# A hybrid decoder layer: two pairs' first products computed ahead of the feed-forward, and pools laid out anew

## The chip, the cores and the metric

The kernel runs on one core of a Trainium2 chip. The metric is the device time of one launch in microseconds (us), as the median of several runs. Four compute engines matter. PE (TensorE) multiplies matrices, and its weight loads (PEld) overlap it. DVE (VectorE), ACT (ScalarE) and POOL (GpSimd) work on elements. SP's queue issues the transfers between HBM and the on-chip memory.

## The reference

The layer works on x of 1024 tokens by 1024 features, in float32:

```python
h = h + jnp.concatenate([o_gla, o_mla], axis=-1) @ w_out[l]      # two groups of heads
h = h + xo.reshape(b, s, XA_HEADS * XA_HEAD_DIM) @ xa_w_o[l]     # attention over 256 memory tokens
fn = rms_norm(h, norm_ffn[l])
g = fn @ ffn_w_gate[l]                                           # 1024 x 2816
g_pad = jnp.pad(g, ((0, 0), (CONV_W - 1, 0), (0, 0)))
cw = ffn_conv_w[l]
g_conv = ffn_conv_b[l] + sum(cw[i] * g_pad[:, i:i + s] for i in range(CONV_W))
h = h + (jax.nn.silu(g_conv) * (fn @ ffn_w_up[l])) @ ffn_w_down[l]
```

## The kernel before

**Arithmetic.** A float32 product is made of three fast ones. Each operand is split into a high part (an ACT copy to the fast type) and a low part (a DVE subtraction), and PE adds low times high, high times low and high times high. `split` does the two halves, `mm3` and `product` the three matmuls.

**Order of stages.** Input projections, gated linear attention and latent attention fill the span to about 483 us, w_out follows, and from about 575 to 717 us runs the cross-attention, a software pipeline over eight tiles of 128 tokens (`for s_ in range(NB + 5)`). Its last stages per tile are `x_o` (output product), `x_fn` (RMS norm) and `x_ft` (transposes and first sums). The feed-forward follows, and from about 1168 us the product with ffn_w_down (`dn`).

**The feed-forward product.** Gate (m_ = 0) and up (m_ = 1) are computed for 11 pairs j of 128-column blocks with a Winograd form of Strassen's scheme, which takes seven block products P1 to P7 instead of eight. The activation's halves are split by features (b1., b2.) and by tokens (tiles 0 to 3, tiles 4 to 7). P1 and P2 use tiles 0 to 3 alone (`fh`, `fl`). P5, P6, P7, P3 and P4 use tiles 4 to 7, and their operands `obP3` to `obP7` are combinations: t1 = b12 - b11 and t2 = b22 - t1 in `x_ft`, t2 - b11 (P7) and t2 - b21 (P4) in `x_t34`. For tiles 4 to 6 these sums run on POOL, for tile 7 on DVE (the variable `ge`). So nothing but P1 and P2 can start before the last tile is through the norm and all its combinations.

**P1 and P2 of pair 0** are therefore computed while the last tiles are worked on, from a separate load of the weights' first 128 columns (`w_first`, tiles hgate, lgate, hup, lup; PSUM tile `A2`, named A).

**The weights** of a pair come as two 1 MB loads (`raw_load`, tile `rw`, one for gate and one for up). `prep` makes the sums of blocks (tile `ss`; on DVE for the first, on POOL for all others) and splits each operand into a tile `op`, seven products ahead (`LA = 7`), in a ring of nine. `run` issues the product's 12 matmuls of 128x512 and adds its result to `GU`. Results of P1 are kept in `p1`.

**What sets the order.** The framework's scheduler orders each engine's instructions by dependences and priority; `pri` shifts the priority. SBUF tiles lie in pools which are stacked from the left and from the right. A tile waits until the last users of its place are done (`reuse_waits="tile"`). So `rw` of the up weights, in pool `rw1`, and the feed-forward's `ss` and `op` tiles wait for the cross-attention's tiles under them.

**Addresses.** The left pools begin 128 bytes past a multiple of 512, because the tile `xsrow` (128 bytes per partition) lies ahead of them. The right pools begin 160 bytes past one, because of the `padr` tile. In the pool of the projections' weights, tiles of 2432 bytes put those behind them at other places again.

Of the kernel before, what the change touches and what calls it, by code (L numbers as in the profile page):

```python
# [33 lines left out]
def build(tc, a, out):  # L34
# [315 lines left out]
    for k in range(KD):  # L350
        raw = xpc.tile([P, 304], F32, name="raw_wv1", tag="raw", bufs=5)
        nc.sync.dma_start(out=raw[:, 0:272], in_=a["w_in"][k * P:(k + 1) * P, C_V + 256:C_OG])
        nc.sync.dma_start(out=raw[:, 272:304], in_=a["w_in"][k * P:(k + 1) * P, C_PE:C_END])
        if k % 2 == 0:
            hi, lo = [pAc.tile([P, 2, 304], F32R, name=f"{nm}_wv1", tag="w", bufs=8) for nm in ("hi", "lo")]
        split(hi[:, k % 2], lo[:, k % 2], raw, col(R_NM + k))
        W.append((hi[:, k % 2], lo[:, k % 2]))
    for t in range(NB):
# [737 lines left out]
        tt(hs, hs, o, ALU.add)  # L1096

    def x_fn(t):
        if not fg:
            fg.append(p4c.tile([P, D], F32, name="fgain"))  # L1100
            nc.sync.dma_start(out=fg[0], in_=a["norm_ffn"].partition_broadcast(P).rearrange("p o n -> p (o n)"))
# [17 lines left out]
    def x_ft(t):  # L1119
# [28 lines left out]
        for nm, src in (("P6", t2), ("P5", t1)):  # L1148
            act(OB[nm][0][:, :, cs], src, AF.Copy)
            tt(OB[nm][1][:, :, cs], src, f32(OB[nm][0][:, :, cs]), ALU.subtract, ge)  # L1150

    def x_t34(nm, t):
# [4 lines left out]
        ge = nc.vector if t == NB - 1 else nc.gpsimd  # L1157
        b = OB["P1" if nm == "P7" else "P2"]
        if t < NB - 1:
            x = p4c.tile([P, 4, P], F32, name="t3", tag="xpT", bufs=2)  # L1160
        else:
            if len(TT) < 2:
                TT.append(qtc.tile([P, 2, 4, P], F32, name="t3b", tag="uB", bufs=1))
            x = TT[1][:, int(nm == "P4")]
        tt(x, T2R[t], f32(b[0][:, :, cs]), ALU.subtract, ge)
        tt(x, x, f32(b[1][:, :, cs]), ALU.subtract, ge)
# [63 lines left out]
    for s_ in range(NB + 5):  # L1230
# [27 lines left out]
        if s_ == 10:
            xvp.__exit__(None, None, None)
            p1p = pool("p1", "right"); p1c = p1p.__enter__()  # L1260
            rwp = [pool("rw0", "right")]
            rwc = [rwp[0].__enter__()]
            raw_load(0, 0)
            for t in range(4, 7):
                x_t34("P7", t)
            W0, A2 = [w_first(i) for i in range(2)], [two(0, [P, 2, 512], "A2")]
            for t in range(4, 7):
                x_t34("P4", t)
            for m_ in range(2):
                product(A2[0][:, m_], W0[m_][0:4], "P1", True)  # L1270
            p1_copy(0)
        if s_ == 11:
            p1_copy(1)
            qps.__exit__(None, None, None)
            x_ft(7)
            for m_ in range(2):
                product(A2[0][:, m_], W0[m_][4:8], "P2", False)
            x_t34("P7", 7)
            x_t34("P4", 7)
    GU = k16([P, 2, 2, S], F32, "GU")  # L1280
# [12 lines left out]
    NP = NF // 2
    ORDER = ("P1", "P6", "P5", "P7", "P2", "P3", "P4")
    prods = [(j, m_, nm) for j in range(NP) for m_ in range(2) for nm in ORDER if j or nm not in ("P1", "P2")]
    OPS, SS, BK, CV = {}, {}, {}, {}

    def prep(j, m_, nm):
# [21 lines left out]
    def conv(f, i):  # L1320

        g_ = GU[:, 0, i]
        c = CV[f] = fcc.tile([P, S], F32, name="conv", tag="conv", bufs=2)
        act(c, g_, AF.Identity, scale=col(R_CW + 2 * NF + f), bias=col(R_CB + f))
        stt(c[:, 1:], g_[:, 0:S - 1], col(R_CW + NF + f), c[:, 1:], ALU.mult, ALU.add)
        stt(c[:, 2:], g_[:, 0:S - 2], col(R_CW + f), c[:, 2:], ALU.mult, ALU.add)
        act(c, c, AF.Silu)

    def run(j, m_, nm):
# [18 lines left out]
        if (nm == "P2" or (j == 0 and nm == "P7")) and m_ == 0:  # L1348
            act(Y[:, 0, 0:512], A2[0][:, 0], AF.Copy)
        if (nm == "P2" or (j == 0 and nm == "P7")) and m_ == 1:  # L1350
            tt(CV[2 * j][:, 0:512], CV[2 * j][:, 0:512], A2[0][:, 1], ALU.mult)
# [114 lines left out]
```

## Time and profile before

| | |
|---|---|
| median of 3 runs | 1414.21 us (1414.16 to 1415.16) |
| the profiled execution | 1413.37 us, span 1411.6 us |
| TensorE clock granted, mean of the span | 0.989 |
| busy PE | 1364.3 us (97%) |
| busy DVE, ACT, POOL | 848.5, 636.8, 231.8 us |

The profile shows one execution. "Busy" counts time in which an engine had an instruction; a matmul's duration includes the time in which it overlaps the next one, so of a row of matmuls the distance between starts (the pitch) tells the speed. Engine idle time carries the instruction that ended it. The granted clock is 1.00 at full speed (2.4 GHz) and 0.50 at half (1.2 GHz).

### The profile page before, as it was taken

To read this page: it belongs to the slowest core of one execution; us is meant where nothing else is said; L and a number is where in the kernel's file an instruction comes from. 1 tells how busy PE (TensorE), PEld (TensorE's weight loads), DVE (VectorE), ACT (ScalarE), POOL (GpSimd) and SP (SyncE) were. 2 spreads that over 40 slices of the span, in tenths; PEclk is the share of its full clock that TensorE was granted. 3 is DMA by queue.
4 is the path that set the end of the run, shared out by engine and by line. 5 is a ranking of instruction groups with operands and counts; after the bars stand their busy time and mean duration, and the time that the engine had idled before them with its cause. 6 is when DMAs were issued, how large, how long until landed. Compare 5 with 4: busy or idle time off the path is not lost.

```text
span 1411.6 us, 19224 instructions
## 1 busy us (share of the span) xinstructions
PE 1364.3 (97%) x7372; PEld 1136.2 (80%) x7372; DVE 848.5 (60%) x1607; ACT 636.8 (45%) x1314; POOL 231.8 (16%) x339
## 2 busy tenths in 40 slices
PE   8999999899999999999966999999999999999998
PEld 8977789788777787888854788888888888888887
DVE  6536785776785624677766766666666656225321
ACT  6424457777776603565433433333333344223220
POOL 0300001222231000000183333222333300000000
PEclk9999999999999999999987999999999999999999
DMA  7111010110001302201012222222222138346521
GB/s 217 47 46 30 9 38 20 53 60 27 2 11 65 135 19 86 76 28 48 31 60 90 90 90 80 70 90 90 90 90 75 45 126 292 109 176 236 180 104 60
DMA packets 69068, 116.11 MB, mean 82 GB/s; under 512 B 6505, under 2 KB 45552, under 8 KB 68976
## 3 DMA queue, kind: packets, MB, share of 16 engines
q1 hardware_dynamic: 68802, 114.82, 24.1%
q8 instruction: 58, 0.95, 0.3%
q14 instruction: 34, 0.28, 0.1%
q10 hardware_dynamic: 174, 0.06, 0.0%
HBM read 94.95 MB, written 19.92 MB: 81 GB/s over the span
## 4 chain that ended last, share of the span: by engine, by line
PE 76%; issue 12%; DVE 4%; POOL 3%; ACT 3%; DMA 2%; SPq 0%; ACTq 0%; DVEq 0%; POOLq 0%
PE dn L1428 6%; PE dn L1429 6%; PE dn L1427 6%; PE P L1212 6%; PE P L1213 6%; PE P L1214 6%; PE pj L88 4%; PE pj L89 4%; PE pj L90 4%; PE mo L756 3%; PE A L1213 3%; PE A L1212 3%; PE A L1214 3%; PE PTp L727 2%; PE S L88 2%
## 5 line engine op out<-in xcount | busy, mean ns | idle before, releaser
L1212 PE MATMUL P<-obP,op 128*128 128x512 f32 x352 | 138.9, 395 | 18.0 <-DVE op L69 12.6
L1214 PE MATMUL P<-obP,op 128*128 128x512 f32 x352 | 138.4, 393 | 0.0
L1213 PE MATMUL P<-obP,op 128*128 128x512 f32 x352 | 138.4, 393 | 0.0
L1427 PE MATMUL dn<-wd,gt 128*128 128x512 f32 x352 | 136.9, 389 | 0.0
L1428 PE MATMUL dn<-wd,gt 128*128 128x512 f32 x352 | 136.9, 389 | 0.0
L1429 PE MATMUL dn<-wd,gt 128*128 128x512 f32 x352 | 136.9, 389 | 0.0
L69 DVE TENSOR_TENSOR wd<-rd,wd 128x1024 fp32r<-128x1024 f32 x44 | 53.0, 1224 | 92.9 <-ACT wd L66 92.9
L66 ACT ACTIVATE op<-ss 128x512 fp32r<-128x512 f32 x88 | 54.8, 630 | 116.9 <-PE P L1214 77.5
L69 POOL TENSOR_TENSOR ss<-rw 128x512 f32<-128x512 f32 x42 | 54.6, 1321 | 268.3 <-DVE op L69 268.3
L69 DVE TENSOR_TENSOR op<-rw,op 128x512 fp32r<-128x512 f32 x62 | 65.5, 1058 | 51.8 <-ACT op L66 51.8
L1212 PEld LDWEIGHTS P<-obP,op 128*128 128x128 f32 x352 | 67.0, 190 | 34.0 <-DVE op L69 13.0
L66 ACT ACTIVATE wd<-rd 128x1024 fp32r<-128x1024 f32 x44 | 45.7, 1058 | 95.9 <-PE dn L1429 49.8
L1214 PEld LDWEIGHTS P<-obP,op 128*128 128x128 f32 x352 | 66.9, 190 | 14.0
L1213 PEld LDWEIGHTS P<-obP,op 128*128 128x128 f32 x352 | 66.9, 190 | 13.9
L1427 PEld LDWEIGHTS dn<-wd,gt 128*128 128x128 f32 x352 | 66.1, 188 | 13.8
L1428 PEld LDWEIGHTS dn<-wd,gt 128*128 128x128 f32 x352 | 66.1, 188 | 13.8
L1429 PEld LDWEIGHTS dn<-wd,gt 128*128 128x128 f32 x352 | 66.1, 188 | 13.5
L66 ACT ACTIVATE op<-rw 128x512 fp32r<-128x512 f32 x62 | 39.0, 631 | 83.7 <-PE P L1214 65.4
L69 DVE TENSOR_TENSOR op<-ss,op 128x512 fp32r<-128x512 f32 x88 | 61.2, 701 | 19.6 <-ACT op L66 18.7
L1212 PE MATMUL A<-fh,op 128*128 128x512 f32 x160 | 62.2, 389 | 0.0
L1213 PE MATMUL A<-fl,op 128*128 128x512 f32 x160 | 62.2, 389 | 0.0
L1214 PE MATMUL A<-fh,op 128*128 128x512 f32 x160 | 62.2, 389 | 0.0
(408 smaller groups left out, 3621.3 us busy)
## 6 DMA issues: line engine op xcount, KB each, us to landing
rd<-in_ffn_w_down SPq DMA_DIRECT2D x44, 512.0 KB
rw<-in_ffn_w_gate SPq DMA_DIRECT2D x11, 1024.0 KB
rw<-in_ffn_w_up SPq DMA_DIRECT2D x11, 1024.0 KB
gdr<-conv SPq DMA_DIRECT2D x22, 512.0 KB
rgd<-gdr SPq DMA_DIRECT2D x44, 256.0 KB
mraw<-in_xa_w_kv SPq DMA_DIRECT2D x16, 256.0 KB
hh<-in_x SPq DMA_DIRECT2D x2, 2048.0 KB
raw_wo<-in_w_out SPq DMA_DIRECT2D x8, 512.0 KB
```

The costliest lines, as they stand in the source:

```text
L66: nc.scalar.activation(out=o, in_=i, func=f, **kw)
L69: (eng or nc.vector).tensor_tensor(out=o, in0=x, in1=y, op=op)
L88: mm(o, lhsT=ll, rhs=rh, start=i == 0, stop=False)
L89: mm(o, lhsT=lh, rhs=rl, start=False, stop=False)
L90: mm(o, lhsT=lh, rhs=rh, start=False, stop=last and i == n - 1)
L756: mm(u.o[r, i], lhsT=V[:, k, x.h * MV:(x.h + 1) * MV], rhs=x.pT[b][:, k - k0], start=k == 0, stop=k == u.t)
L1212: mm(o, lhsT=wl, rhs=bh[:, k], start=start and k == 0, stop=False, **kw)
L1213: mm(o, lhsT=wh, rhs=bl[:, k], start=False, stop=False, **kw)
L1214: mm(o, lhsT=wh, rhs=bh[:, k], start=False, stop=k == 3, **kw)
L1427: mm(ob[b], lhsT=gl, rhs=wh, start=f == 0, stop=False)
L1428: mm(ob[b], lhsT=gh, rhs=wl, start=False, stop=False)
L1429: mm(ob[b], lhsT=gh, rhs=wh, start=False, stop=f == NF - 1)
```

## The change

1. Before the feed-forward, a second pair's P1 and P2 are computed too. `w_first` takes the pair as argument; for pair 1 it splits the weights into a 16 KB tile `wx`. Four products (48 matmuls) write two PSUM pairs `x1p`, and P1 and P1 + P2 are kept in `X1`. Pair 1's P1 and P2 are gone from `prods`, with their splits. The loads of `w_first` are issued at steps 8 and 9 of the cross-attention and after it, instead of at step 10.
2. `x_t34` becomes `x_t234` with an engine argument. P6's part for tiles 4 and 5 stays on POOL, and for 6 on goes to DVE. P7's and P4's parts run on DVE for every tile, in the order 7, 6, 5, 4, those of P4 for tiles 5 and 4 later than the rest.
3. Pools are opened in another order. Conv tiles and three `op` tiles lie in `fc`, `ss` in `fs`, the rest in `rg`. The ring has seven `op` tiles up to pair 2, nine after. The look-ahead is six products for pairs 0 and 1 and eight after.
4. `xsrow` lies inside `alr`, `padr` grows from 320 to 480 bytes, and the 2432-byte weight tiles become 2560 bytes. All SBUF tiles of 1 KB and more then begin at a multiple of 512 bytes.

```diff
-    padr.tile([P, 80], F32, name="padr", tag="padr", bufs=1)
+    padr.tile([P, 120], F32, name="padr", tag="padr", bufs=1)
...
-    xsrow = const.tile([P, NB, XH], F32, name="xsrow")
+    xsrow = alr[:, :, 0:XH]
...
-            hi, lo = [pAc.tile([P, 2, 304], F32R, name=f"{nm}_wv1", tag="w", bufs=8) for nm in ("hi", "lo")]
+            hi, lo = [pAc.tile([P, 640], F32R, name=f"{nm}_wv1", tag="w", bufs=8)[:, 0:608].rearrange("p (k n) -> p k n", k=2) for nm in ("hi", "lo")]
...
-        ge = nc.vector if t == NB - 1 else nc.gpsimd
+        ge = nc.vector if t >= NB - 2 else nc.gpsimd
...
+        if j:
+            if not WX:
+                WX.append(k16([P, 2, 2, KD, P], F32R, "wx"))
+            hi, lo = WX[0][:, i, 0], WX[0][:, i, 1]
+            split(hi, lo, raw)
+            return [(hi[:, k], lo[:, k]) for k in range(KD)]
...
+    for m_ in range(2):
+        product(A2[0][:, m_], WF[m_, 0][0:4], "P1", True)
+        p1_copy(m_)
+    product(A2[0][:, 0], WF[0, 0][4:8], "P2", False)
+    x_t234("P6", 4, nc.gpsimd)
+    x_t234("P6", 5, nc.gpsimd)
+    x_ft(7)
+    x_t234("P6", 6, nc.vector)
+    x_t234("P6", 7, nc.vector)
+    product(A2[0][:, 1], WF[1, 0][4:8], "P2", False)
+    for nm in ("P7", "P4"):
+        for t in (7, 6, 5, 4):
+            with pri(-200 if nm == "P4" and t < 6 else 0):
+                x_t234(nm, t, nc.vector)
...
+    RING = [(rgc, "op0"), (rgc, "op1")] + RING + [(rgc, "op5"), (rgc, "op6")]
...
+    xb_ = [[fpc.tile([P, 512], F32, name="x1p", tag=f"{nm}{m_}", bufs=1) for m_ in range(2)] for nm in ("P6", "P5")]
+    for i, nm in enumerate(("P1", "P2")):
+        for m_ in range(2):
+            product(xb_[i][m_], WF[m_, 1][4 * i:4 * i + 4], nm, True)
+            if i == 0:
+                act(X1[0][:, m_], xb_[0][m_], AF.Copy)
+            else:
+                tt(X1[1][:, m_], X1[0][:, m_], xb_[1][m_], ALU.add)
...
-    prods = [(j, m_, nm) for j in range(NP) for m_ in range(2) for nm in ORDER if j or nm not in ("P1", "P2")]
+    prods = [(j, m_, nm) for j in range(NP) for m_ in range(2) for nm in ORDER if j > 1 or nm not in ("P1", "P2")]
...
+        while done < min(len(prods), i + (6 if x[0] < 2 else 8)):
+            with pri(250 if done < 2 else 0):
+                prep(*prods[done])
+            done += 1
```

On PE, at the place where the last product that needs tiles 0 to 3 alone is followed by the first that needs tile 7, before (A is pair 0's P2, `P` and `D` are PSUM tiles, `op` a split weight operand; 8058 is obP6):

```order
L1212 MATMUL A_8264<-fh,lup 128x512
L1213 MATMUL A_8264<-fl,hup 128x512
L1214 MATMUL A_8264<-fh,hup 128x512
L1212 MATMUL P_8414<-obP_8058,op 128x512
L1213 MATMUL P_8414<-obP_8058,op 128x512
L1214 MATMUL P_8414<-obP_8058,op 128x512
```

The same place now (x1p is a product of pair 1; 8349 is obP4, 8290 obP6):

```order
L1220 MATMUL x1p<-fh,wx 128x512
L1221 MATMUL x1p<-fl,wx 128x512
L1222 MATMUL x1p<-fh,wx 128x512
L1220 MATMUL D_8561<-obP_8349,op 128x512
L1221 MATMUL D_8561<-obP_8349,op 128x512
L1222 MATMUL D_8561<-obP_8349,op 128x512
L1220 MATMUL D_8561<-obP_8349,op 128x512
L1221 MATMUL D_8561<-obP_8349,op 128x512
L1220 MATMUL P_8485<-obP_8290,op 128x512
```

The join is now between pair 1's ahead-computed products and five matmuls of P4, where it was between A and P6. Ahead of it stand 84 matmuls of A and x1p after the cross-attention's last one, where 32 stood.

On DVE, from tile 7's last low part of P5 to the first weight sums, before (t3b is tile 7's P7 or P4 combination):

```order
L69 TENSOR_TENSOR obP_8057<-t_8059,obP_8057 128x4x128
L69 TENSOR_TENSOR t3b<-t_8319,fh 128x512
L69 TENSOR_TENSOR obP_8058<-t_8319,obP_8058 128x4x128
L69 TENSOR_TENSOR t3b<-t3b,fl 128x512
L69 TENSOR_TENSOR t3b<-t_8319,fh 128x512
L69 TENSOR_TENSOR t3b<-t3b,fl 128x512
L69 TENSOR_TENSOR obP_8232<-t3b,obP_8232 128x4x128
L69 TENSOR_TENSOR obP_8265<-t3b,obP_8265 128x4x128
L69 TENSOR_TENSOR ss<-rw 128x512 x2
```

The end of the corresponding piece now (8349 is obP4; t_8354, t_8359 and t_8364 are its combinations for tiles 6, 5 and 4):

```order
L69 TENSOR_TENSOR ss<-ss,rw 128x512
L69 TENSOR_TENSOR obP_8349<-t_8354,obP_8349 128x4x128
L69 TENSOR_TENSOR op<-ss,op 128x512
L69 TENSOR_TENSOR ss<-rw,ss 128x512
L69 TENSOR_TENSOR op<-rw,op 128x512
L69 TENSOR_TENSOR t_8359<-t_8150,fh 128x512
L69 TENSOR_TENSOR op<-ss,op 128x512
L69 TENSOR_TENSOR t_8359<-t_8359,fl 128x512
L69 TENSOR_TENSOR t_8364<-t_8058,fh 128x512
L69 TENSOR_TENSOR t_8364<-t_8364,fl 128x512
L69 TENSOR_TENSOR obP_8349<-t_8359,obP_8349 128x4x128
L69 TENSOR_TENSOR obP_8349<-t_8364,obP_8349 128x4x128
```

The weights' sums and splits now stand among the last combinations of P4, instead of behind all of them. From the instruction that makes tile 7's t1 to the last obP4, DVE has 34 instructions of 128x512; POOL's part of the stage shrinks from 27 instructions to 6.

## Rows read from the trace of the kernel before

**Rows 1.** The page: busy tenths and granted clock in 40 slices, costliest group.

```profile
PE   8999999899999999999966999999999999999998
PEclk9999999999999999999987999999999999999999
L1212 PE MATMUL P<-obP,op 128*128 128x512 f32 x352 | 138.9, 395 | 18.0 <-DVE op L69 12.6
```

**Rows 2.** Windows: us, then busy (count) of PE, PEld, DVE, ACT, POOL, clock, DMA.

```profile
580.00:720.00 140.00, 137.20 (x811) 118.83 (x809) 100.89 (x210) 80.29 (x200) 16.26 (x12) 1.00 0.15 53
...
720.00:737.00 17.00, 9.68 (x32) 7.06 (x32) 14.46 (x15) 5.16 (x11) 16.26 (x13) 0.70 0.00 0
737.00:750.00 13.00, 0.38 (x2) 0.33 (x2) 9.18 (x13) 5.26 (x10) 5.37 (x5) 0.62 0.25 81
```

**Rows 3.** Timeline of PE: start, us, line, out<-in [idle before <-releaser].

```profile
716.38 0.39 PE L90 MATMUL xo<-woh,xo 128*128 128x512 f32 x1
...
724.39 0.80 PE L1212 MATMUL A<-fh,lgate 128*128 128x512 f32 x1 [4.90 <-ACT p L66]
...
728.48 1.09 PE L1129 MATMUL tp<-ident,fn 128*128 128x128 f32 x4 [2.86 <-DVE fn L72]
...
749.67 0.79 PE L1212 MATMUL P<-obP,op 128*128 128x512 f32 x1 [12.62 <-DVE op L69]
750.27 0.63 PE L1213 MATMUL P<-obP,op 128*128 128x512 f32 x1
...
753.68 0.50 PE L1212 MATMUL P<-obP,op 128*128 128x512 f32 x1
...
767.21 0.52 PE L1212 MATMUL P<-obP,op 128*128 128x512 f32 x1 [3.10 <-DVE GU L69]
...
804.74 0.39 PE L1213 MATMUL D<-obP,op 128*128 128x512 f32 x1
...
808.60 0.39 PE L1212 MATMUL P<-obP,op 128*128 128x512 f32 x1
```

**Rows 4.** Timeline of DVE, tile 7's norm and combinations.

```profile
716.81 0.69 DVE L69 TENSOR_TENSOR hh<-hh,xo 128x512 f32<-128x512 f32 x1 [0.22 <-PE xo L90]
...
720.92 0.15 DVE L161 TENSOR_SCALAR ra_m<-mss 128x1 f32<-128x1 f32 x1
...
724.16 1.20 DVE L72 SCALAR_TENSOR_TENSOR ra_t<-ra_t,ra_m 128x1 f32<-128x1 f32 x1
...
731.21 0.69 DVE L69 TENSOR_TENSOR t<-tp,fh 128x512 f32<-128x512 f32 x1 [1.21 <-PE tp L1129]
...
735.80 1.78 DVE L69 TENSOR_TENSOR t3b<-t,fh 128x512 f32<-128x512 f32 x1
...
742.85 0.68 DVE L69 TENSOR_TENSOR t3b<-t3b,fl 128x512 f32<-128x512 f32 x1
743.45 0.68 DVE L69 TENSOR_TENSOR t3b<-t,fh 128x512 f32<-128x512 f32 x1
744.16 0.69 DVE L69 TENSOR_TENSOR t3b<-t3b,fl 128x512 f32<-128x512 f32 x1
```

**Rows 5.** Timeline of POOL, its last combinations and the first weight sums.

```profile
739.88 2.49 POOL L69 TENSOR_TENSOR obP<-t,obP 128x512 fp32r<-128x512 f32 x2
751.50 2.90 POOL L69 TENSOR_TENSOR ss<-rw 128x512 f32<-128x512 f32 x2 [9.13 <-DVE op L69]
```

**Rows 6.** SP's queue: the load of pair 0's up weights, and the next.

```profile
744.19 0.38 SPq L1223 DMA_DIRECT2D rw<-in_ffn_w_up  x1
752.06 0.38 SPq L1223 DMA_DIRECT2D rw<-in_ffn_w_gate  x1
```

**Rows 7.** Timeline of PE in w_out, two products of 12.

```profile
486.76 0.39 PE L89 MATMUL pj<-lo_wo,oh 128*128 128x512 f32 x1
...
488.58 0.40 PE L88 MATMUL pj<-hi_wo,ol 128*128 128x512 f32 x1
...
491.38 0.40 PE L88 MATMUL pj<-hi_wo,ol 128*128 128x512 f32 x1
```

More of the change, by code (lines that the diff above doesn't have):

```diff
@@ L1098, in x_fn @@
     def x_fn(t):
-        if not fg:
-            fg.append(p4c.tile([P, D], F32, name="fgain"))
-            nc.sync.dma_start(out=fg[0], in_=a["norm_ffn"].partition_broadcast(P).rearrange("p o n -> p (o n)"))
         xn = qtc.tile([P, D], F32, name="fn", tag="qt", bufs=3)
@@ L1134, in x_ft @@
         if t == 4:
-            for nm in ("P3", "P5", "P6"):
+            for nm in ("P3", "P5"):
                 o_ = k16([P, 2, 4, 512], F32R, f"ob{nm}")
@@ L1147, in x_ft, with x_t234 @@
         tt(OB["P3"][1][:, :, cs], b22, f32(OB["P3"][0][:, :, cs]), ALU.subtract)
[L1148 to L1152, printed above, removed]
+        act(OB["P5"][0][:, :, cs], t1, AF.Copy)
+        tt(OB["P5"][1][:, :, cs], t1, f32(OB["P5"][0][:, :, cs]), ALU.subtract, ge)
+    def x_t234(nm, t, ge):
         if nm not in OB:
@@ L1156, in x_t34 @@
         cs = slice((t % 4) * P, (t % 4 + 1) * P)
[L1157 to L1160, printed above, removed]
-        else:
[L1162 to L1166, printed above, removed]
+        if nm == "P6":
+            x = T2R[t]
+        else:
+            b = OB["P1" if nm == "P7" else "P2"]
+            if t < NB - 1:
+                x = p4c.tile([P, 4, P], F32, name="t3", tag="xpT", bufs=2)
+            else:
+                if len(TT) < 2:
+                    TT.append(qtc.tile([P, 2, 4, P], F32, name="t3b", tag="uB", bufs=1))
+                x = TT[1][:, int(nm == "P4")]
+            tt(x, T2R[t], f32(b[0][:, :, cs]), ALU.subtract, ge)
+            tt(x, x, f32(b[1][:, :, cs]), ALU.subtract, ge)
         act(OB[nm][0][:, :, cs], x, AF.Copy)
@@ L1183, in build, with w_first @@
     p4 = pool("p4"); p4c = p4.__enter__()
-    fg = []
+    fg = [p4c.tile([P, D], F32, name="fgain")]
+    nc.sync.dma_start(out=fg[0], in_=a["norm_ffn"].partition_broadcast(P).rearrange("p o n -> p (o n)"))
     def ok(t):
         return 0 <= t < NB
-    def w_first(i):
+    def w_first(i, j):
         raw = p3c.tile([P, KD, P], F32, name="raw_f", tag="raw", bufs=1)
-        nc.sync.dma_start(out=raw, in_=a[("ffn_w_gate", "ffn_w_up")[i]][:, 0:P].rearrange("(k p) n -> p k n", p=P))
+        nc.sync.dma_start(out=raw, in_=a[("ffn_w_gate", "ffn_w_up")[i]][:, 2 * P * j:2 * P * j + P].rearrange("(k p) n -> p k n", p=P))
+        if j:
[4 more added lines that the diff above has]
+            return [(hi[:, k], lo[:, k]) for k in range(KD)]
         if i == 0:
@@ L1197, in w_first @@
         r = []
-        for j in range(2):
+        for h in range(2):
             hi, lo = [p3c.tile([P, 4, P], F32R, name=nm, tag=tg, bufs=2) for nm, tg in (("hup", "hnh"), ("lup", "hnl"))]
-            split(hi, lo, raw[:, 4 * j:4 * j + 4])
+            split(hi, lo, raw[:, 4 * h:4 * h + 4])
             r += [(hi[:, k], lo[:, k]) for k in range(4)]
         return r
+    WX, WF = [], {}
     def product(o, ws, nm, start):
@@ L1257, in build @@
             x_ft(s_ - 4)
[L1258 to L1280, printed above, removed]
+        if s_ == 8:
+            WF[0, 0] = w_first(0, 0)
+        if s_ == 9:
+            WF[1, 0] = w_first(1, 0)
+            WF[0, 1] = w_first(0, 1)
+    xvp.__exit__(None, None, None)
+    p1p = pool("p1", "right"); p1c = p1p.__enter__()
+    rwp = [pool("rw0", "right")]
+    rwc = [rwp[0].__enter__()]
+    raw_load(0, 0)
+    WF[1, 1] = w_first(1, 1)
+    A2 = [two(0, [P, 2, 512], "A2")]
+    for m_ in range(2):
[12 more added lines that the diff above has]
+                x_t234(nm, t, nc.vector)
+    qps.__exit__(None, None, None)
     p4.__exit__(None, None, None)
@@ L1283, in build @@
     qtp.__exit__(None, None, None)
+    fcp = pool("fc"); fcc = fcp.__enter__()
+    for i in range(2):
+        fcc.tile([P, S], F32, name="conv", tag=f"conv{i}", bufs=1)
+    RING = [(fcc, "op2"), (fcc, "op3"), (fcc, "op4")]
+    for pl, tg in RING:
+        pl.tile([P, 2, 4, P], F32R, name="op", tag=tg, bufs=1)
     fsp = pool("fs"); fsc = fsp.__enter__()
-    fcp = pool("fc"); fcc = fcp.__enter__()
+    fsc.tile([P, 4, 4, P], F32, name="ss", tag="ss", bufs=1)
     rgp = pool("rg"); rgc = rgp.__enter__()
+    for tg in ("op0", "op1"):
+        rgc.tile([P, 2, 4, P], F32R, name="op", tag=tg, bufs=1)
+    X1 = [rgc.tile([P, 2, 512], F32, name="x1", tag=f"op{i}", bufs=1) for i in (7, 8)]
+    RING = [(rgc, "op0"), (rgc, "op1")] + RING + [(rgc, "op5"), (rgc, "op6")]
     rwp.append(pool("rw1", "right"))
@@ L1292, in build @@
     raw_load(0, 1)
+    xb_ = [[fpc.tile([P, 512], F32, name="x1p", tag=f"{nm}{m_}", bufs=1) for m_ in range(2)] for nm in ("P6", "P5")]
[4 more added lines that the diff above has]
+                act(X1[0][:, m_], xb_[0][m_], AF.Copy)
+            else:
+                tt(X1[1][:, m_], X1[0][:, m_], xb_[1][m_], ALU.add)
+    GU = k16([P, 2, 2, S], F32, "GU")
     NP = NF // 2
     ORDER = ("P1", "P6", "P5", "P7", "P2", "P3", "P4")
-    prods = [(j, m_, nm) for j in range(NP) for m_ in range(2) for nm in ORDER if j or nm not in ("P1", "P2")]
+    prods = [(j, m_, nm) for j in range(NP) for m_ in range(2) for nm in ORDER if j > 1 or nm not in ("P1", "P2")]
     OPS, SS, BK, CV = {}, {}, {}, {}
@@ L1313, in prep @@
             src = SS[j, m_][:, {"P5": 0, "P6": 1, "P7": 2, "P3": 3}[nm]]
-        o = rgc.tile([P, 2, 4, P], F32R, name="op", tag="op", bufs=9)
+        if (j, m_, nm) == (2, 1, "P1"):
+            RING.extend([(rgc, "op7"), (rgc, "op8")])
+        pl, tg = RING.pop(0)
+        RING.append((pl, tg))
+        o = pl.tile([P, 2, 4, P], F32R, name="op", tag=tg, bufs=1)
         split(o[:, 0], o[:, 1], src)
@@ L1322, in conv @@
         g_ = GU[:, 0, i]
-        c = CV[f] = fcc.tile([P, S], F32, name="conv", tag="conv", bufs=2)
+        c = CV[f] = fcc.tile([P, S], F32, name="conv", tag=f"conv{f % 2}", bufs=1)
         act(c, g_, AF.Identity, scale=col(R_CW + 2 * NF + f), bias=col(R_CB + f))
@@ L1343, in run @@
         if nm == "P6":
+            if j == 1:
+                PA[m_] = X1[0][:, m_]
             tt(Y[:, 0, 512:], PA[m_], bk, ALU.add)
@@ L1347, in run @@
             tt(Y[:, 1, 512:], Y[:, 1, 0:512], BK["P5"], ALU.add)
[L1348 to L1351, printed above, removed]
+        if nm == ("P2" if j > 1 else "P7"):
+            c11 = X1[1][:, m_] if j == 1 else A2[0][:, m_]
+            if m_ == 0:
+                act(Y[:, 0, 0:512], c11, AF.Copy)
+            else:
+                tt(CV[2 * j][:, 0:512], CV[2 * j][:, 0:512], c11, ALU.mult)
         if nm == "P3":
@@ L1367, in run @@
                 nc.sync.dma_start(out=gdr[2 * j + 1], in_=c)
-    LA = 7
-    for x in prods[0:LA]:
-        prep(*x)
+    done = 0
     for i, x in enumerate(prods):
+        while done < min(len(prods), i + (6 if x[0] < 2 else 8)):
+            with pri(250 if done < 2 else 0):
+                prep(*prods[done])
+            done += 1
         run(*x)
-        if i + LA < len(prods):
-            prep(*prods[i + LA])
     fps.__exit__(None, None, None)
@@ L1439, in build @@
     fsp.__exit__(None, None, None)
+    fcp.__exit__(None, None, None)
     es.close()
```

1 line of the change is left out of this document (removed).

## The prediction

> **What bounds the kernel now.** I read the page's slices first. PE is busy 97% of the span, and its one hollow is in slices 20 and 21, where the granted clock drops too [rows 1]. The windows put it between 720 and 750 us: in 13 us from 737 on PE works 0.38 us [rows 2]. PE's timeline gives the waits. After the cross-attention's last matmul (716.38) PE waits 4.90 us, then 2.86 us for tile 7's normalised rows, then 12.62 us for the first product that needs tile 7, and 3.10 us inside pair 0 [rows 3]. The last also shows what a wait leaves behind: from 750.27 to 753.68 the starts are 0.426 us apart (8 steps), and from 804.74 to 808.60 0.227 (17 steps), which are the half and the full level of the clock.
>
> I count what the stretch needs. From 716.38 to 749.67 (33.3 us) it holds the last output matmul and 32 of A, at 0.227 is 7.5 us, and 16 transposes. Four of those last 1.09 us at half clock [rows 3], so 16 at full are 2.2 us. Lost: 23.6 us. From 749.67 to 808.60, where pair 1's P6 of the up half begins, the program has 216 matmuls, 49.0 us of 58.9; lost: 9.9 us. So 33.5 us is all that can be won here.
>
> Who ends last in the gap? DVE makes tile 7's t1 only at 731.21, 14.4 us after its add at 716.81. The norm's small instructions, 0.15 us when left alone, take up to 1.20 us there, and a 512-wide combination takes 1.78 us where others follow each other every 0.60 [rows 4]. POOL runs all that time: 16.26 of the 17 us up to 737 [rows 2], and its last combination lasts until 742.4 [rows 5].
>
> **The change part by part.**
>
> *Pair 1's P1 and P2 ahead.* 48 matmuls at 0.227 are 10.9 us of the same work at another time, so by itself it costs PE nothing. After the cross-attention PE then has 84 matmuls (19.1 us) and the transposes (2.2 us). The waits of 4.90 and 2.86 us are filled. Four of the 84 stood ahead of 716.38 before; their 0.9 us I leave out on both sides. PE runs out at about 716.6 + 21.3 = 737.9. The extra splits (2 instructions of twice the width on ACT and on DVE) and the two extra 512 KB loads lie in a stage where PE is busy 137.20 of 140 us while DVE has 39 us free [rows 2]; I cost them at nothing. If that cover failed it would be their own DVE time, 2 x 2 x 0.6 = 2.4 us. Pair 1 sheds as many splits later.
>
> *Combinations from POOL to DVE.* Until tile 7's t1 DVE has 12 instructions of 512 width or the like (0.60 each) and 5 small ones (0.15), 8.0 us from 716.8, and half a microsecond for the transposes: t1 at 725.3. Then 34 instructions up to the last part of P4's operand, 34 x 0.60, and 0.11 more for some five that read what the one before wrote (743.45 to 744.16 against 742.85 to 743.45, [rows 4]): 21.0 us, so 746.3. Five matmuls of P4 are now first in PE's row behind the ahead-computed ones, and they wait for that; P6, ready sooner, stands behind them and waits too. The gap is 746.3 - 737.9 = 8.4 us instead of 12.62. Bounds: if the six instructions left on POOL hold up the five small ones as before (1.20 each), 5.3 us more; if the scheduler's waits are met exactly and DVE's last four weight splits slip behind P4, 2.4 us less.
>
> A rule bears on this. The Trainium skill, page *SBUF — State Buffer*, section *Who interferes with whom*, says that DVE and GpSimd share one port pair, and that an instruction of one with two inputs from SBUF shuts out the other's reads for its whole length. The 1.78 us beside 0.60 agree with it. By it alone the six POOL instructions could each hold DVE for one of their durations (half of 2.49, [rows 5]), 7.5 us in all, and the gap would be 15.9 us.
>
> *Clock after the gap.* 749.67 to 753.68 are 9 matmuls in 4.0 us instead of 2.0. I take the same 2.0 us (0 if the shorter gap leaves the clock up, 4.0 for twice as many).
>
> *Pair 0's other waits.* Of the 9.9 us lost after 749.67, 7.9 remain without that restart: 3.10 us of wait, others like it, and their half clock. The order P4, P7, P3 ahead of P6 and P5 readies weights while the last combinations are being made, but the ring is shorter (7) and the look-ahead too (6). I take half, 4.0 us (0 to 7.9). The load of pair 0's up weights, issued at 744.19 and used by POOL 7.3 us later [rows 5, 6], now stands behind the gate load of pair 1 on SP. That one needs the gate buffer, read for the last time about eight instructions before the end of DVE's row, so some 5 us before 746.3. Both then go out near 741 us. With 7.3 us each in line the up weights are there at 756, two POOL sums (1.25 us each) and a split later at 760. PE reaches them after 60 matmuls and the restart, 746.3 + 13.6 + 2.0 = 762. Hidden, by 2 us.
>
> *Pair 2.* There P1 and P2 return and the look-ahead grows by two: two operands must be made beyond those used, 2 x 2 x 0.6 = 2.4 us on ACT and DVE in turn. I take 2.5 us, between 0 (slack suffices) and 5.
>
> *Addresses.* In w_out the same loop runs at two pitches: 486.76 to 488.58 8 steps of 0.2275, then 488.58 to 491.38 12 steps of 0.2333 [rows 7]. In the second the two operands lie at different places past a multiple of 512 bytes (one in a left, one in a right pool), in the first at the same; the feed-forward's, both in left pools, run at 0.227 [rows 3]. If that is the cause, a mixed pair costs 6 ns. By the loops, 1,152 matmuls of 512 width stand ahead of the feed-forward (384 in w_out, 192 each in the output product, the cross-attention's queries and the gated attention's inputs, 144 and 48 in latent attention). All mixed: 6.9 us. I take half, 3.5 us; bounds 0 and 6.9. Here the skill speaks against me: the same section says that only that shared pair contends and that PE waits for nobody at SBUF. By it this term is 0, which is the second rival.
>
> *Nothing else.* `fgain` and the pool at the end move no work on the path.
>
> **Sum.** Lost after: 8.4 + 2.0 + 4.0 + 2.5 = 16.9 us. Gain 33.5 - 16.9 = 16.6, and 3.5 for the addresses: 20.1 us. The profiled execution took 1413.37 us (1411.6 of span), so 1393.3; the median lies 0.84 above it: 1394 us.
>
> **The rivals.**
>
> *Addresses count for nothing* (the pitches differ for another reason, such as the restart after a short wait): the 3.5 us go, 1397.6 us. For it: one loop with two pitches is little evidence. Against: the pitch changes inside an unbroken row.
>
> *The up weights come late.* The 2 us of cover go if SP waits longer for the gate buffer, and each load time is 7.3 us. PE then waits once more in the middle of pair 0, about 7 us: 1401 us. For it: SP's order, two loads where one stood. Against: the cover as worked out.
>
> *Pair 0 runs through.* With weights made ahead the 4.0 and the 2.5 us vanish: 1387.5 us. Against: fewer buffers.
>
> *DVE becomes the bound (slower).* All combinations now go through DVE, and if each of the 34 paid what rows of before show at their worst (1.78 us), the operand of P4 would be 40 us late. The decision lies at 0.60 + 20.1/34 = 1.19 us each. At 1.25 it gives 34 x 0.65 = 22 us more: 1416 us. For it: the rows of 1.78 and 1.20. Against: they stand beside POOL's instructions, of which 21 of 27 go, and the bare pace beside an idle POOL is 0.60.
>
> *Given back.* The 48 matmuls are only moved, and if pairs 1 and 2 then stall on their operands by as much as the gap lost, nothing stays: 1413 us. Against: pair 1 has two sevenths fewer operands to make.
>
> **How the numbers follow.** Forecast 0.49 (1394), addresses nothing 0.25 (1397.6), late up weights 0.10 (1401), pair 0 runs through 0.07 (1387.5), DVE the bound 0.05 (1416), given back 0.04 (1413). The bounds of the single terms do not fall together; gap and start-up give about 7 us to either side, the addresses 3.5. The range 1385 to 1403 holds the first four cases and leaves out the rest of 0.09 and the tails. A difference under 0.2% (2.8 us) cannot be told from no change here. Faster 0.91, same 0.04, slower 0.05.
>
> **What would show it.** Right: no wait on PE between 717 and 737 us; one wait of 7 to 10 us before a `D` matmul released by DVE; t1 of tile 7 near 725 us; DVE's combinations 0.6 us apart; equal pitches of 0.227 in w_out. Wrong: a long wait behind the first `D` or `P` matmuls with DVE's instructions over 1 us (DVE the bound), a wait on POOL's `ss` in the middle of pair 0 (late weights), idle rows on PE after pair 1 (given back), or pitches of 0.233 left in w_out.

## The result and the profile after

| | before | changed |
|---|---|---|
| median | 1414.59 us (1414.16 to 1415.16, 4 runs) | 1398.45 us (1397.98 to 1399.09, 4 runs) |
| ratio | | 0.9888, 95% interval 0.9876 to 0.9901 |
| profiled execution's span | 1411.6 us | 1396.3 us |
| TensorE clock, mean | 0.989 | 0.994 |

The change takes 16.1 us off; 20.1 were forecast (1394 us). The time lies in the range, and nearer to the rival in which the addresses count for nothing (1397.6). That nearness is chance: the addresses do count, as the runs below show, and most of what is missing is lost elsewhere.

The page of the changed kernel answers to [rows 1]. The hollow is narrower, and the wait ahead of the costliest group has fallen from 18.0 us to 3.8, in part because the long wait now stands before a `D` matmul, in another group:

```profile
PE   8999999899999999999997999999999999999998
...
PEclk9999999999999999999998999999999999999999
...
L1220 PE MATMUL P<-obP,op 128*128 128x512 f32 x352 | 139.2, 395 | 3.8 <-DVE GU L69 3.7
```

PE's timeline of the changed kernel (start, us, line, out<-in, idle before) answers to [rows 3]:

```profile
714.53 0.39 PE L90 MATMUL xo<-woh,xo 128*128 128x512 f32 x1
715.35 1.07 PE L1126 MATMUL tp<-ident,fn 128*128 128x128 f32 x8 [0.43 <-DVE fn L72]
...
720.59 0.50 PE L1220 MATMUL A<-fh,lgate 128*128 128x512 f32 x1 [0.52 <-ACT p L66]
...
736.82 0.39 PE L1222 MATMUL x1p<-fh,wx 128*128 128x512 f32 x1
744.79 0.80 PE L1220 MATMUL D<-obP,op 128*128 128x512 f32 x1 [7.58 <-ACT obP L66]
...
750.38 0.40 PE L1221 MATMUL P<-obP,op 128*128 128x512 f32 x1
...
773.99 0.50 PE L1220 MATMUL P<-obP,op 128*128 128x512 f32 x1 [0.90 <-DVE GU L69]
...
832.48 0.39 PE L1222 MATMUL P<-obP,op 128*128 128x512 f32 x1
834.83 0.50 PE L1220 MATMUL P<-obP,op 128*128 128x512 f32 x1 [1.96 <-DVE GU L69]
...
839.28 0.40 PE L1220 MATMUL A<-fh,op 128*128 128x512 f32 x1
```

In place of the waits of 4.90 and 2.86 us stand two of 0.43 and 0.52, the long one is 7.58 us instead of 12.62, and it stands before a `D` matmul of P4. From 744.79 to 750.38 (granted clock 0.50) twelve steps take 5.59 us, 2.9 more than at full clock. There is a wait that the kernel before did not have, at 834.83 in pair 2. With its half clock it costs 3.9 us (13 steps from 832.48 to 839.28 in 6.80 us instead of 2.95).

DVE of the changed kernel answers to [rows 4], POOL and SP to [rows 5, 6]:

```profile
724.61 0.69 DVE L69 TENSOR_TENSOR t<-tp,fh 128x512 f32<-128x512 f32 x1
...
743.99 1.47 DVE L69 TENSOR_TENSOR obP<-t,obP 128x512 fp32r<-128x512 f32 x2
```

```profile
748.91 1.28 POOL L69 TENSOR_TENSOR ss<-rw 128x512 f32<-128x512 f32 x1 [30.94 <-DMA rw<-in_ffn_w_up]
```

```profile
741.01 0.38 SPq L1231 DMA_DIRECT2D rw<-in_ffn_w_gate  x1
741.62 0.41 SPq L1231 DMA_DIRECT2D rw<-in_ffn_w_up  x1
```

Tile 7's t1 starts 10.1 us after the cross-attention's last matmul (14.8 before), the last part of obP4 ends at 745.46, and POOL, waiting for the up weights, goes on at 748.91.

### The profile page after: what moved, and what is told of

Its sections match the earlier page's. It is cut to its first block, busy times and chain, and to the rows that moved or that the text cites. A ratio compares the mean times of both kernels' runs of the same rounds, so it can differ in the third digit from the quotient of the medians.

```text
span 1396.3 us, 19231 instructions
## 1 busy us (share of the span) xinstructions
PE 1361.8 (98%) x7372; PEld 1135.5 (81%) x7372; DVE 853.7 (61%) x1628; ACT 636.2 (46%) x1312; POOL 203.9 (15%) x318
## 4 chain that ended last, share of the span: by engine, by line
PE 85%; DVE 7%; issue 3%; ACT 3%; DMA 1%; POOL 0%; SPq 0%; ACTq 0%; DVEq 0%; POOLq 0%
PE pj L88 6%; PE pj L89 6%; PE pj L90 6%; PE dn L1470 6%; PE dn L1471 6%; PE dn L1469 6%; PE P L1220 6%; PE P L1221 5%; PE P L1222 5%; PE mo L756 3%; PE PTp L727 2%; PE A L1220 2%; PE A L1221 2%; PE A L1222 2%; PE S L88 2%
## 5 line engine op out<-in xcount | busy, mean ns | idle before, releaser
L66 ACT ACTIVATE wd<-rd 128x1024 fp32r<-128x1024 f32 x44 | 45.6, 1056 | 97.8 <-PE dn L1471 50.1
L69 DVE TENSOR_TENSOR op<-rw,op 128x512 fp32r<-128x512 f32 x58 | 62.6, 1079 | 42.6 <-ACT op L66 42.5
L1471 PEld LDWEIGHTS dn<-wd,gt 128*128 128x128 f32 x352 | 66.1, 188 | 13.6
L1470 PEld LDWEIGHTS dn<-wd,gt 128*128 128x128 f32 x352 | 66.1, 188 | 13.6
L72 DVE SCALAR_TENSOR_TENSOR conv<-GU,cols,conv 128x1023 f32<-128x1023 f32 (+1 forms) x44 | 56.9, 1298 | 3.7 <-ACT conv L66 3.3
L717 DVE TENSOR_REDUCE mx<-S 128x1 f32<-128x128 f32 (+7 forms) x64 | 48.1, 752 | 15.5 <-PE S L715 15.2
L1220 PE MATMUL A<-fh,op 128*128 128x512 f32 x144 | 56.0, 389 | 0.0
```

The lines of the kernel that those rows point to most:

```text
L72: nc.vector.scalar_tensor_tensor(out=o, in0=x, scalar=s, in1=y, op0=op0, op1=op1)
L1220: mm(o, lhsT=wl, rhs=bh[:, k], start=start and k == 0, stop=False, **kw)
L1470: mm(ob[b], lhsT=gh, rhs=wl, start=False, stop=False)
L1471: mm(ob[b], lhsT=gh, rhs=wh, start=False, stop=f == NF - 1)
```

## The experiments

PE's rows give four stretches for each kernel: up to the last score matmul `S`, from there to w_out's last (`pj<-hi_wo`), from there to the cross-attention's last (`xo`), and from there to the first `dn`. The first spreads over 3.1 us from one execution to the next whatever the kernel. w_out and the cross-attention stay within 0.4 us among kernels with like addresses. The feed-forward lies between: 450.1 to 452.2 us in the first three kernels of the table, which run the same matmuls in it in the same order. The rest of this section leans on these later stretches.

| kernel | median | to S | w_out | cross-att. | feed-forward |
|---|---|---|---|---|---|
| before | 1414.59 | 474.31 | 99.43 | 142.64 | 451.50 |
| addr_only | 1411.16 | 473.37 | 97.81 | 142.38 | 452.22 |
| addr_128 | 1410.98 (one run) | 474.84 | 97.91 | 142.61 | 450.11 |
| combos_dve | 1407.98 | 475.02 | 99.51 | 142.51 | 445.54 |
| changed | 1398.45 | 474.24 | 97.75 | 142.54 | 437.92 |
| addr_undone | 1400.17 | 476.48 | 99.44 | 142.65 | 436.59 |
| combos_pool | 1405.87 | 474.41 | 97.86 | 142.56 | 444.46 |
| one_pair | 1407.58 | 474.04 | 97.86 | 142.64 | 447.94 |
| look6 | 1399.55 | 474.94 | 98.12 | 142.59 | 438.08 |
| look678 | 1398.30 | 475.42 | 97.83 | 142.63 | 438.02 |
| filler24 | 1397.06 | 473.96 | 97.86 | 142.75 | 437.06 |
| ring_front | 1398.28 | 475.71 | 98.10 | 142.66 | 438.11 |
| ring_filler | 1397.77 | 475.29 | 97.93 | 142.63 | 436.76 |
| sums_dve | 1395.01 | 475.29 | 97.78 | 142.64 | 434.29 |

**Addresses alone, and undone.** `addr_only` is the kernel before with the three lines of part 4, `addr_undone` the changed kernel without them. `addr_128` gives both sides' operands a common place 128 bytes past a multiple of 512:

```diff
-    padr.tile([P, 80], F32, name="padr", tag="padr", bufs=1)
+    padr.tile([P, 88], F32, name="padr", tag="padr", bufs=1)
...
+            hi, lo = [pAc.tile([P, 640], F32R, name=f"{nm}_wv1", tag="w", bufs=8)[:, 0:608].rearrange("p (k n) -> p k n", k=2) for nm in ("hi", "lo")]
```

> The kernel before with part 4 alone (all large tiles at multiples of 512 bytes). Theory (addresses count a little: the pitch of 0.233 us in w_out falls to 0.227, but only where PE is the bound, so 1 to 2 us of the 16): 1412.6 to 1413.6 us against 1414.6 of before. Rival (they count as forecast, 3.5 us): 1411. Rival (nothing; the change of pitch in the changed kernel has another cause): 1414.6, with both pitches still in w_out.

> The changed kernel with part 4 undone. Theory: the mixed pitches of w_out come back, 1 to 2 us slower than the changed kernel's 1398.5, 1399.5 to 1400.5. Rival (3.5 us): 1402. Rival (nothing): 1398.5.

> The kernel before with the right pools and the 2432-byte tiles moved so that operands of both sides begin 128 bytes past a multiple of 512 (128, not 0). Theory (what counts is that the two operands of a matmul lie at the same place): w_out takes 97.8 us from the last score matmul S to its own last, as with part 4, where before took 99.4; pitches 0.227. Rival (multiples of 512 count): 99.4 us, pitches up to 0.233.

`addr_only` took 0.9981 of before's time (0.9973 to 0.9990): 1.4 to 3.8 us less, and 3.1 by the medians, near the larger of the two sizes expected. Undone, the ratio to before is 0.9903 (0.9889 to 0.9917) instead of 0.9888, which is 2.1 us, the intervals overlapping. So the medians don't decide between the sizes; the rows show where the time goes. These are w_out's two ends (last S, last pj) in before, in the changed kernel and in `addr_128`:

```profile
474.31 0.40 PE L90 MATMUL S<-KTh,QT 96*128 96x512 f32 x1
...
573.74 0.40 PE L90 MATMUL pj<-hi_wo,oh 128*128 128x512 f32 x1
```

```profile
474.24 0.40 PE L90 MATMUL S<-KTh,QT 96*128 96x512 f32 x1
...
571.99 0.39 PE L90 MATMUL pj<-hi_wo,oh 128*128 128x512 f32 x1
```

```profile
474.84 0.40 PE L90 MATMUL S<-KTh,QT 96*128 96x512 f32 x1
...
572.75 0.40 PE L90 MATMUL pj<-hi_wo,oh 128*128 128x512 f32 x1
```

The stretch is 99.43 to 99.51 us in the three kernels with the old addresses and 97.75 to 98.12 in the eleven with a common place, 1.6 us. Only half of its 384 matmuls are mixed: the weights of 192 lie in a right pool, 160 bytes past a multiple of 512, those of the other 192 in a left one, 128 bytes past, as all activations do. From before to the changed kernel the mean step falls from 234 to 227 ns in the first half and from 230 to 227 in the second, where before's first few steps behind a mixed row are slow too ([rows 7], from 491.38 on).

A second stage shows the same. In this unbroken row of the input projections all operands of before begin at multiples of 128 bytes, the activations 128 past a multiple of 512, the weights, behind tiles of 2432 bytes, at 0, 128, 256 or 384. First before, then `addr_128`:

```profile
97.50 0.40 PE L88 MATMUL pj<-xh,lo_wq 128*128 128x512 f32 x1
...
116.40 0.40 PE L88 MATMUL pj<-xh,lo_wq 128*128 128x512 f32 x1
```

```profile
97.06 0.39 PE L88 MATMUL pj<-xh,lo_wq 128*128 128x512 f32 x1
...
115.42 0.39 PE L88 MATMUL pj<-xh,lo_wq 128*128 128x512 f32 x1
```

81 steps take 18.90 us (0.2333 each), then 18.36 (0.2267). So the common place need not be a multiple of 512 (`addr_128`), and it isn't enough that each operand begins at a multiple of 128 (this row). What the fast rows have in common is that the two operands lie alike; whether by 512 bytes or by 256, no run tells. The rival "nothing" is out. The feed-forward, whose operands lie alike in before already, is not shorter with the new addresses (437.92 against 436.59, 452.22 against 451.50). In `addr_undone` it is shorter because the clock recovers sooner: 7 slow steps after the long gap instead of 12, and none after the wait in pair 2.

**One pair ahead.** The changed kernel without wx and x1p, pair 1 computing all seven products:

```diff
-    WF[1, 1] = w_first(1, 1)
...
-    prods = [(j, m_, nm) for j in range(NP) for m_ in range(2) for nm in ORDER if j > 1 or nm not in ("P1", "P2")]
+    prods = [(j, m_, nm) for j in range(NP) for m_ in range(2) for nm in ORDER if j > 0 or nm not in ("P1", "P2")]
```

> The changed kernel without the second pair ahead: pair 1 computes its own P1 and P2 as before, no wx, no x1p. Theory (PE runs out of work 48 x 0.227 = 10.9 us earlier while DVE's row ends when it did): the wait before the first D matmul grows from 7.6 to about 18 us, and the time to 1409 us, less up to 4 us if the stall at the look-ahead's step goes too. Rival (the combinations' move alone makes the gain, the moved products only fill time that is lost later): 1399 us, with new waits missing in pairs 1 and 2.

1407.58 us (1407.09 to 1408.54), ratio 0.9957 (0.9943 to 0.9970). Its PE rows at the join:

```profile
725.50 0.39 PE L1222 MATMUL A<-fh,hup 128*128 128x512 f32 x1
743.45 0.80 PE L1220 MATMUL D<-obP,op 128*128 128x512 f32 x1 [17.55 <-ACT obP L66]
```

The gap is 17.55 us. The 48 matmuls fill it and are not lost again: the feed-forward is 10.0 us longer without them (10.9 us of matmuls).

**Combinations back on POOL, and on DVE alone.** `combos_pool` is the changed kernel with the engine choice of before; `combos_dve` is the kernel before with the engine alone changed. The lines are those of `combos_dve`:

```diff
-        ge = nc.vector if t == NB - 1 else nc.gpsimd
+        ge = nc.vector if t >= NB - 2 else nc.gpsimd
...
-        ge = nc.vector if t == NB - 1 else nc.gpsimd
+        ge = nc.vector
```

> The changed kernel with the combinations of tiles 4 to 6 back on POOL, as before. Theory (POOL's row of 21 instructions at 1.25 to 1.5 us from about 717 us on ends between 743 and 749, and slows DVE's small instructions beside it, so tile 7's t1 comes 3 to 6 us later): the first D matmul at 748 to 752 instead of 744.8, 1402 to 1406 us. Rival (DVE's row is as long as POOL's, the move only swaps engines): 1398 to 1399 us.

> The kernel before with the combinations of tiles 4 to 6 for P7 and P4, and P6's and t1's part of tile 6, on DVE instead of POOL, in the old order, and nothing else. Theory (POOL's long row of sums held DVE's small instructions of tile 7's norm; without it t1 comes near 725 instead of 731, then some 27 instructions at 0.6 us to the first weight split): the first P matmul about 28 us after the cross-attention's end, where it was 33.3, and 1408 to 1411 us against 1414.5. Rival (DVE's row grows by what POOL's shrinks): 1414 us or more.

`combos_pool` took 1405.87 us (1404.70 to 1407.77), `combos_dve` 1407.98 (1406.99 to 1408.30; ratio 0.9956, 0.9943 to 0.9968). In the first, DVE's rows are as slow as before's and PE waits 13.12 us:

```profile
724.09 3.39 DVE L72 SCALAR_TENSOR_TENSOR fn<-hh,nr,fgain 128x512 f32<-128x512 f32 x2
...
738.88 3.44 DVE L69 TENSOR_TENSOR t3b<-t,fh 128x512 f32<-128x512 f32 x2
```

```profile
754.02 0.77 PE L1220 MATMUL P<-obP,op 128*128 128x512 f32 x1 [13.12 <-DVE op L69]
```

In the second, the norm's small instructions are back at 0.15 us, and the first P matmul comes 27.1 us after 717.04, where it came 33.3 us after:

```profile
723.05 0.15 DVE L72 SCALAR_TENSOR_TENSOR ra_t<-ra_t,ra_m 128x1 f32<-128x1 f32 x1
```

```profile
717.04 0.39 PE L90 MATMUL xo<-woh,xo 128*128 128x512 f32 x1
...
744.17 0.79 PE L1212 MATMUL P<-obP,op 128*128 128x512 f32 x1 [13.03 <-DVE op L69]
```

So moving 21 instructions from POOL (339 before, 318 after) onto the engine that ended last makes that engine finish earlier: each engine's instructions slow the other's when both run. DVE's are the rows above; POOL's sum of 128x512 takes 2.26 us beside DVE (827.00 below) and 1.28 at 748.91, where DVE is idle. The rival "the move only swaps engines" is out both ways, by 6.0 and 6.5 us of the feed-forward stretch.

**The wait in pair 2.** The look-ahead was suspected first, then the ring of `op` places, then the sums on POOL:

```diff
-        while done < min(len(prods), i + (6 if x[0] < 2 else 8)):
+        while done < min(len(prods), i + 6):                                          # look6
+        while done < min(len(prods), i + (6 if x[0] < 2 else 7 if x[0] < 3 else 8)):  # look678
...
-            RING.extend([(rgc, "op7"), (rgc, "op8")])
+            RING[0:0] = [(rgc, "op7"), (rgc, "op8")]                                  # ring_front
...
-        ge = nc.vector if j == 0 and m_ == 0 else nc.gpsimd
+        ge = nc.vector if (j, m_) in ((0, 0), (3, 0)) else nc.gpsimd                  # sums_dve
```

> The changed kernel with a look-ahead of six for all pairs instead of six and then eight. Theory (the wait of 1.96 us and its half clock at 834.8 come from the step from six to eight, which crowds ACT's and DVE's queues with two more splits): the wait goes, 1394.5 to 1396 us. Rival (it comes from P1 and P2 returning in pair 2, or from pair 2's weights landing late): the wait stays, 1398 to 1399. Second rival (six is too few with seven products a half): new waits in every pair, over 1400.

> The changed kernel with the look-ahead raised in two steps, six for pairs 0 and 1, seven for pair 2, eight after. Theory: each step adds one split ahead of the copies that PE waits for, so the wait of 1.96 us shrinks to under 1 us, 1395 to 1397 us. Rival (returning products or late weights): 1398 to 1399.

> The changed kernel with the two op places that come free in pair 2 put at the head of the ring instead of its end, so that the splits of pair 2's second half need not wait for places that PE still reads (819.97 waits for the A product's end now). Theory (the wait of 1.96 us at 834.8 comes from that ring of seven: late split, late ss on POOL, late p on ACT, late GU): POOL's sums for pair 3 start some 5 us before 823.5, the wait and its half clock go, 3.5 us, 1395 us. Rival (it comes from the conv work that stands ahead of the p copy on ACT and DVE, after two pairs of short halves): wait unchanged, 1398 to 1399 us.

> The changed kernel with the four weight sums of pair 3's gate half on DVE instead of POOL. Theory (the wait of 1.96 us at 834.8 hangs on these sums: POOL begins them at 823.5 and takes 7.5 us with DVE beside it, ACT's split waits for them, and the copy of P1 and GU's sum stand behind that split): on DVE they take 2.4 us, the split comes some 4 us earlier, and wait and half clock go, 3.5 us: 1395 us. Rival (DVE's own queue holds them up, or the wait moves to another half as it did with the ring): 1398 to 1400 us.

`look6` (1397.26 to 1400.33) and `look678` (1397.59 to 1399.43) kept the wait, 1.96 us in both, so the step of the look-ahead is not its cause. `one_pair` has it too (1.96 us, at 844.75), although its pair 1 computes all seven products, so the moved products are not its cause either. `ring_front` (1396.46 to 1400.10) lost it and got another half a pair earlier:

```profile
818.12 0.80 PE L1220 MATMUL P<-obP,op 128*128 128x512 f32 x1 [2.57 <-DVE GU L69]
```

`sums_dve` took 1395.01 us (1394.43 to 1395.82), ratio 0.9865 (0.9850 to 0.9880), and has no wait there. In the changed kernel, POOL, ACT and DVE read one after the other:

```profile
827.00 2.26 POOL L69 TENSOR_TENSOR ss<-ss,rw 128x512 f32<-128x512 f32 x1
```

```profile
829.29 0.64 ACT L66 ACTIVATE op<-ss 128x512 fp32r<-128x512 f32 x1 [3.92 <-POOL ss L69]
...
831.92 0.58 ACT L66 ACTIVATE p<-A 128x512 f32<-128x512 f32 x1
```

```profile
834.10 0.68 DVE L69 TENSOR_TENSOR GU<-p,P 128x512 f32<-128x512 f32 x1
```

and in `sums_dve` ACT and PE:

```profile
828.53 0.60 ACT L66 ACTIVATE p<-A 128x512 f32<-128x512 f32 x1 [2.09 <-PE A L1222]
...
831.11 1.67 ACT L66 ACTIVATE op<-ss 128x512 fp32r<-128x512 f32 x3
```

```profile
834.98 0.50 PE L1220 MATMUL P<-obP,op 128*128 128x512 f32 x1
```

ACT works in order. In the changed kernel a split of pair 3 stands ahead of P1's copy `p` and waits 3.92 us for POOL's sum; DVE's sum that frees PE's buffer waits for the copy. With the sums elsewhere the scheduler also put the copy first, at once behind P1 (2.09 us waiting for PE only), and the feed-forward is 3.6 us shorter. Two things changed with that edit, the engine of four sums and the order on ACT; the run does not tell which of them is enough. By the median the version is the fastest of all; its runs and the changed kernel's don't overlap.

**The long gap filled.** 24 or 32 more matmuls, whose results are overwritten, behind x1p; `ring_filler` has `ring_front`'s ring too:

```diff
+    dz = two(1, [P, 2, 512], "D2")
+    for i in range(24):
+        mm(dz[:, i % 2], lhsT=WF[0, 1][0][0], rhs=fh[0][:, 0], start=True, stop=True)
```

> The changed kernel with 24 more matmuls of 128x512 without use behind the x1p products, into PSUM that P4's first product overwrites: 5.4 us of the 7.58 us gap is filled. Theory (the clock falls to its half level in the long gap and 2.9 us are lost after it): with a gap of 2.1 us the clock stays up and the D matmuls start at full pitch, 1395 to 1396 us. Rival (the half clock follows any wait of 2 us or more, as at 834.8): pitches of 0.43 remain, 1398 to 1399 us. Second rival (the filler delays the D matmuls): over 1399.

> The same with 32 matmuls without use in the long gap (7.3 of its 7.58 us). Theory (with the 2.1 us wait gone too, the D matmuls start at full clock): no pitch of 0.43 between 744 and 752, 2.9 us less than ring_front, 1392 us if that works, 1395.5 if its ring does nothing. Rival (half clock comes all the same): as ring_front, or 1397 with the wait at 834.8 still there.

`filler24`: 1397.06 us (1394.90 to 1397.57); a wait of 2.14 us is left, and the half clock still comes. `ring_filler`: 1397.77 us (1396.10 to 1398.14); with 0.33 us left, it doesn't. The rows of the one, then of the other:

```profile
744.82 0.50 PE L1220 MATMUL D<-obP,op 128*128 128x512 f32 x1 [2.14 <-ACT obP L66]
...
746.49 0.63 PE L1221 MATMUL D<-obP,op 128*128 128x512 f32 x1
```

```profile
746.11 0.49 PE L1220 MATMUL D<-obP,op 128*128 128x512 f32 x1 [0.33 <-ACT obP L66]
...
747.18 0.39 PE L1222 MATMUL D<-obP,op 128*128 128x512 f32 x1
747.41 0.39 PE L1220 MATMUL D<-obP,op 128*128 128x512 f32 x1
```

With the gap filled the half clock is gone, but the feed-forward gains 1.4 us against `ring_front`, not 2.9, and the medians 0.5, the runs overlapping: PE waits longer on the other engines in pair 0 (0.86 and 0.43 us, where `ring_front` has one wait of 0.33). Nor does a wait's length alone tell whether the clock falls. `addr_128` has the row below in pair 0 and runs on at a granted clock of 1.00, and so does `addr_undone` after 1.98 us in pair 2, where the changed kernel falls to half clock after 1.96.

```profile
766.14 0.50 PE L1212 MATMUL P<-obP,op 128*128 128x512 f32 x1 [3.09 <-DVE GU L69]
```

## Why the prediction was right, point by point

- *Products ahead fill the gap.* Right. PE ran out of work 22.5 us after the start of the cross-attention's last matmul (21.5 forecast; the difference is the waits of 0.43 and 0.52 us), and taking them back costs 9.1 us by the medians.
- *DVE's row to the end of obP4.* Right in mechanism and size: from t1 34 instructions took 20.9 us (21.0). t1 came 10.1 us after the cross-attention (8.9). The gap was 7.58 us (8.4). ACT's half of the operand ended it, not DVE's as forecast; DVE's last part was done 0.7 us later, when the second `D` matmul began.
- *Clock after the gap.* 2.9 us, 2.0 forecast: twelve steps, not nine. The length of the slow stretch varies: after the same gap of 7.6 us it was 7 steps in `addr_undone` and 14 in `ring_front`.
- *Pair 0's and 1's other waits.* 0.53, 0.90 and 0.28 us, with slow first steps about 3 us (4.0). The loads went out at 741, as worked out, and the up weights were there at 748.9, not 756: in my bound each load took 7.3 us, but two issued 0.6 us apart were both done in 7.9 (from 749 on the transfer engines are idle).
- *Pair 2.* The failed step. 3.9 us instead of 2.5, and not because the look-ahead grows or P1 and P2 return: with six throughout the wait was the same, and in `one_pair` too, where they return a pair earlier. What stands there is ACT's order, a split of pair 3 ahead of the copy that PE waits for, held by POOL's sums; which of the two would have to change is open, as said. About half of the 3.9 us is the half clock, which did not follow the same wait in `addr_undone`.
- *Addresses.* The mechanism was right: the pitch goes with the places, in two stages. The size is not settled. 3.5 us were forecast; the whole kernel gave 1.4 to 3.8 in one comparison and about 2 in the other, w_out alone 1.6. The half in the forecast was a guess, and that it came near is luck. By the pools, 496 of the 1,152 matmuls are mixed: 192 in w_out and 304 in the projections, none in the output product and the cross-attention's queries. At 6 ns that is an estimate of 3.0 us. The page *SBUF — State Buffer* of the Trainium skill (section *Who interferes with whom*) says that PE never waits on anyone, by which the term would be zero. The stretch of 99.4 against 97.8 us is not zero; what within PE or SBUF makes the difference no run shows.
- *The same section's rule on POOL and DVE* had the trace behind it, and the exchange of engines agrees with it: 0.15 us instead of 1.20 for the norm's small instructions once POOL is free. The six instructions left on POOL did not hold DVE up by the 7.5 us that the prediction worked out from it: the gap was 7.58 us, not 15.9.
- *Nothing else on the path.* Not quite. Four matmuls of A (0.9 us) moved out of the cross-attention's stretch, which is nevertheless as long as before (142.54 against 142.64). The prediction left those 0.9 us out on both sides. Two waits take most of them up, 0.96 us where before had 0.42, and 0.52 where it had none. `one_pair`, without pair 1's splits and loads, has both waits too, so these are not the cause; `combos_dve` has neither in this length. The cause stays open. First before, then the changed kernel:

```profile
703.84 1.16 PE L1077 MATMUL XO<-xpT,xv 128*128 128x128 f32 x8 [0.42 <-DVE xpT L1067]
```

```profile
702.10 1.16 PE L1077 MATMUL XO<-xpT,xv 128*128 128x128 f32 x8 [0.96 <-DVE xpT L1067]
...
709.18 0.50 PE L88 MATMUL xo<-woh,xo 128*128 128x512 f32 x1 [0.52 <-DVE xo L69]
```

Summed: 7.6 + 2.9 + 3 + 3.9 and about 1 us of small waits ahead of the gap are 18.4 us lost, where 16.9 were forecast. Counted over the whole feed-forward stretch, as its length less its matmuls at 0.227 us and its transposes, 19.3 us are lost, and 33.8 were before. Of the 14.5 us won the four moved matmuls use 0.9, so the stretch is 13.6 us shorter. w_out is 1.7 us shorter and the rest 0.2, together 15.4, by which the two profiled executions differ (1413.37 and 1397.98); the medians differ by 16.1. So of the 20.1 us forecast 3.0 are missing in the feed-forward and about 1.6 in the addresses.

The three parts taken away one by one cost 9.1 (products), 7.4 (engine) and 1.7 us (addresses) by the medians, together 18.2, which is more than the whole 16.1. So some part is worth more beside the others than alone; the runs don't show which. The pools and the ring (part 3) and the new order with P4 first were not taken away by themselves.

## What to carry to other kernels

Where two elementwise engines work side by side ahead of a join, moving all of the work to the faster one can end earlier than sharing it: count the rows in which each slows the other. Work that needs no late input can fill such a gap at almost its full worth (10.0 of 10.9 us here). A wait that is new elsewhere need not come from the moved work: look at the order of the queues, here a split that blocked the copy behind it. And where one loop runs at two pitches, compare the places of the operands before looking for waits.

## What the runs showed of the hardware that was not expected

A matmul's pitch depends on the places of its two operands: with different remainders by 512 bytes w_out took 99.4 us, with the same remainder, 0 or 128, 97.8 to 98.1, and a row of 81 steps in the projections 18.90 us and 18.36. And after a wait of 2.14 us, with full clock ahead of it, TensorE began at full pitch and then ran at a granted clock of 0.50 (0.43 us a step from 746.49 to 749.05, `filler24`). After one of 0.33 us it didn't (`ring_filler`), and not after one of 3.09 us in `addr_128` either.
